# Two-way gated scan inside an encoder layer: inputs asked one place sooner, keys scaled in place, small copies on GpSimd, outputs scaled a place later

## The chip, the cores and the metric

The kernel runs on one core of one Trainium2 chip. The metric is device time in microseconds: the median of three runs, taken without the profiler. One further execution was profiled; all rows of the trace come from it.

The engines are TensorE (PE, with PEld for its weight loads), VectorE (DVE), ScalarE (ACT), GpSimd (POOL) and SyncE (SP). Each works through its own queue in order. SP issues most of the DMA transfers, ACT and GpSimd issue some.

## The reference

One layer of an encoder over 1024 positions of width 1024, all in float32. Cut to what matters:

```python
h = _rmsnorm(x, attn_norm_w)
glu_in, q, v, z_f, z_b, og, g_a, g_b = split(einsum("bsd,de->bse", h, w_in))
a = silu(layernorm(dwconv31(glu(glu_in)))) @ conv_pw_w
o = _bi_hgrn2(q, v, z_f, z_b, lb_fwd, lb_bwd)      # 8 heads of 128
b = (rms_per_head(o) * norm_w * silu(og)) @ hgrn_o_w
x = x + (sigmoid(g_a) * a + sigmoid(g_b) * b) @ w_out
x = x + conv_glu_ffn(rmsnorm(x)) ; out = rmsnorm(x)
```

The scan, in each direction and for each head, with `f = lb + (1 - lb) * sigmoid(z)` clamped to [1e-6, 1] and the key `k = (1 - lb) * sigmoid(-z)`:

```python
S_t = diag(f_t) S_{t-1} + k_t v_t^T
o_t = S_t^T (silu(q_t) * 128**-0.5)
```

The outputs of the forward and the backward scan are added.

## The kernel before

Every large product is done as three passes of float32r matmuls (`mm3`, lines 148 to 150: high by high, high by low, low by high), 128x128 weights against 128x512 activations, contracted over 128 at a time. TensorE's order is the order of the program text. The other engines' queues, SP's and GpSimd's transfers among them, are ordered before the launch by a scheduler that works with estimated costs and with the waits on tiles and pages (a page is one buffer of a tile's ring); instructions that are pinned keep their program order.

The stage around the change is the scan, which runs while the last columns of the input projection and the convolution's output product go on as a stream of dense pieces (`dense`). Work is cut into 16 half-heads: item i is head i // 2, half i % 2, with 512 positions on the free axis, 128 channels on the partitions. For each item:

- `scan_inputs(i)` (lines 1150 to 1166) loads q and two gate inputs z, makes from each z on ACT the key `kG = sigmoid(-z)` (L1162), `sigmoid(z)` (L1163) and `f` (L1164), and clamps f on DVE (L1165). Rings: q 2 pages, f 2, kG 3, z 3. The scale of the keys, `(1 - lb) * 128**-0.5`, comes back as `kscale`, not yet applied.
- `scan_base` is a generator of five steps. The first (lines 1221 to 1246) applies the key scale: `k_d`, the sum of the two scaled keys, by L1223 and L1224, and four half-width products of q, scale and f by L1229, into Q1 and qF. ACT copies kG in woven order (L1175) for the first level; then the keys and queries are doubled: at block size h each is multiplied by the product of the gates of the neighbouring block (`tt`, all recorded at L1143). Later steps do sizes 2, 4, 8 and 16 and issue the first levels of the score matrix on PE (L1194, bank sc).
- `scan_levels` yields three times: levels 8 and 16 (L1194, bank ob) and block 32 (L1284); then nothing; then block 64, after which ACT copies the scores into S (L1312), and four transfers of 16 KB, issued by ACT, put the diagonal 32x32 blocks D into S (L1314).
- `scan_states` yields twice: PE transposes kG (L1324), ACT copies them into kT (L1326), PE makes the states (L1333), and DVE chains the forward ones (L1339, L1341).
- The outputs of a head are a stream called `pending`, which runs during the next head: backward states (L1426); output products of half 0 (L1374), their copy on ACT and the sums of squares (L1379); the same of half 1, then on GpSimd the mean and the power to -0.5 (L591, L592, tile ors); an empty step; scaling on ACT of half 0, then half 1 (L1393, eight instructions of a quarter half); transposes and gating of half 0, then half 1 (L1400, L1402), stored to DRAM, or, for the last head, split into two parts for the output product.

The order is written out in the loop of lines 1449 to 1490. After each of an item's five yields `between(n)`, n = 0 to 4, runs: these are the five places. A place advances the dense stream by 1.77 pieces on average (a piece is six matmuls), `pending` by one step and the base of the next item (n below 4) or the one after it (n = 4) by one step. The inputs of item i + 2 are asked at the start of item i, that is, behind place 4 of item i - 1. Before the loop items 0 and 1 are asked, seven dense pieces follow, and then the steps of item 0's base with dense pieces between them.

Behind the loop `TAIL` gives the last head's outputs six steps with dense pieces between them; then come the loads of the other heads' outputs for half 0, one more step, the rest of the dense stream, the loads for half 1 and the last step. The output product `o_jobs` follows, head by head, so that the last head's first half is its eighth operand.

Of the kernel before, what the change touches and what calls it, by code (L numbers as in the profile page):

```python
# [18 lines left out]
P = 128  # L19
# [12 lines left out]
H = 512  # L32
# [5 lines left out]
def view(t, off, dims):  # L38

    return bass.AP(  # L40
        tensor=t.tensor,
        offset=t.offset + off,
        ap=[list(t.ap[0])] + [list(d) for d in dims],
    )
# [3 lines left out]
def tile_hybrid_encoder(  # L48
# [45 lines left out]
    def nm(s):  # L94
        uid[0] += 1
        return f"{s}_{uid[0]}"
# [6 lines left out]
    def page(pool, tag, bufs, dt=F32):  # L103
        return pool.tile([P, H], dt, tag=tag, name=nm(tag), bufs=bufs)
# [1046 lines left out]
    def scan_inputs(i):  # L1151


        h, half = divmod(i, 2)
        q = page(hp, "q", 2)
        f = hp.tile([P, 2, H], F32, tag="f", name=nm("f"), bufs=2)
        kG = hp.tile([P, 2, H], F32, tag="kG", name=nm("kG"), bufs=3)
        nc.sync.dma_start(q, d_q[h][half])
        for d in range(2):
            z = page(hp, "zi", 3)  # L1160
            nc.sync.dma_start(z, d_z[d][h][half])
            A.activation(kG[:, d, :], z, AF.Sigmoid, scale=-1.0)  # L1162
            A.activation(z, z, AF.Sigmoid)  # L1163
            A.activation(f[:, d, :], z, AF.Identity, scale=oml_of(d, h), bias=lb_of(d, h))  # L1164
        V.tensor_scalar(f, f, MIN_FORGET, 1.0, op0=ALU.max, op1=ALU.min)  # L1165
        return q, f, kG, kscale[:, h : h + NH + 1 : NH]
# [49 lines left out]
    def scan_base(ins):  # L1216


        q, f, kG, ks = ins
        qF = hp.tile([P, 2, H], F32, tag="qF", name=nm("qF"), bufs=4)  # L1220
        D_t = hp.tile([P, 4, 32], F32, tag="D", name=nm("D"), bufs=3)
        k_d, Q1 = page(hp, "A", 8), page(hp, "A", 8)
        V.tensor_scalar(k_d, kG[:, 1, :], ks[:, 1:2], None, op0=ALU.mult)  # L1223
        V.scalar_tensor_tensor(k_d, kG[:, 0, :], ks[:, 0:1], k_d, op0=ALU.mult, op1=ALU.add)  # L1224
        A1 = woven(kG, 1)
        odd = H // 2

        def gated(to, at, t, d):
            V.scalar_tensor_tensor(  # L1229
                view(to, at, [[2, odd]]),  # L1230
                view(q, t, [[2, odd]]),
                ks[:, d : d + 1],
                view(f, d * H + t, [[2, odd]]),
                op0=ALU.mult,
                op1=ALU.mult,
            )

        for t in range(2):
            gated(Q1, t, t, 1 - t)
        for t in (1, 0):  # L1240
            gated(qF, (1 - t) * H + t, t, t)
        double_keys(kG, f, 1)
        double_queries(qF, pairs(Q1, 1, 0), f, 1)
        tb = totals(f, 1)
        yield
        A2, Q2 = woven(kG, 2), woven(qF, 2)
        double_keys(kG, tb, 2)
        double_queries(qF, pairs(qF, 2), tb, 2)
        tb = totals(tb, 2)
        A4, Q4 = woven(kG, 4), woven(qF, 4)  # L1250
        yield
        b = bank("sc")
        for n, (k_t, q_t) in enumerate(((k_d, q), (A1, Q1), (A2, Q2), (A4, Q4))):
            level(slot(b, n), k_t, row(q_t))
        double_keys(kG, tb, 4)
        double_queries(qF, pairs(qF, 4), tb, 4)
        tb = totals(tb, 4)
        A8, Q8 = woven(kG, 8), woven(qF, 8)
        yield
        A.copy(D_t, near(slot(b, 3)))  # L1260
        for n, m in enumerate((m_d, m_1, m_2)):
            V.copy_predicated(D_t, over(m), near(slot(b, n)))
        double_keys(kG, tb, 8)
        double_queries(qF, pairs(qF, 8), tb, 8)
        tb = totals(tb, 8)
        A16, Q16 = woven(kG, 16), woven(qF, 16)
        yield
        double_keys(kG, tb, 16)
        double_queries(qF, pairs(qF, 16), tb, 16)
        tb = totals(tb, 16)  # L1270
        yield qF, kG, tb, D_t, A8, Q8, A16, Q16

    def scan_levels(base, S_t, Tt):


        qF, kG, tb, D_t, A8, Q8, A16, Q16 = base

        def blocks(b, h):

            for c in range(0, H, P):  # L1280
                for s0 in range(0, P, h):
                    t0 = s0 ^ h
                    d = s0 // h % 2
                    T.matmul(  # L1284
                        b[s0 : s0 + h, c + t0 : c + t0 + h],
                        kG[:, d, c + s0 : c + s0 + h],
                        qF[:, 1 - d, c + t0 : c + t0 + h],
                        start=True,
                        stop=True,
                    )  # L1290

        def double(tb, h, to=None):
            double_keys(kG, tb, h)
            double_queries(qF, pairs(qF, h), tb, h)
            return totals(tb, h, to)

        b = bank("ob")
        level(slot(b, 0), A8, row(Q8))
        level(slot(b, 1), A16, row(Q16))
        S_b = bank("sc")  # L1300
        for at, g, _ in each():
            T.matmul(S_b[g, at : at + 32], none, none, start=True, stop=True)
        blocks(S_b, 32)
        for n, m in enumerate((m_8, m_16)):
            V.copy_predicated(D_t, over(m), near(slot(b, n)))
        tb = double(tb, 32)
        yield
        yield
        b = S_b
        blocks(b, 64)  # L1310
        double(tb, 64, view(Tt, 0, [[4, 2], [1, 4]]))
        A.copy(S_t, c4(b))  # L1312
        for g in range(0, P, 32):
            nc.scalar.dma_start(S_t[g : g + 32, :, g : g + 32], D_t[g : g + 32])  # L1314
        yield

    def scan_states(i, kG, v, Tt, Sf, Sb):
# [38 lines left out]
    def scan_outputs(h, kept, Sf, Sb):  # L1356


        ons, gates = [], []
        ss = cp.tile([P, 2, 4], F32, name=nm("oss"), tag="oss", bufs=2)  # L1360
        rs = cp.tile([P, 2, 4], F32, name=nm("ors"), tag="ors", bufs=2)
        for half in range(2):
            S_t, v, qF = kept[half]
            o = bank("ob")
            for c in range(4):
                sl = slice(c * P, (c + 1) * P)
                g = half * 4 + c
                terms = [(S_t[:, c, :], v[:, c, :])]
                if g > 0:
                    terms.append((qF[:, 1, sl], Sf[half][:, c, :]))  # L1370
                if g < 7:
                    terms.append((qF[:, 0, sl], Sb[half][:, c, :]))
                for n, (l, r) in enumerate(terms):
                    T.matmul(o[:, sl], l, r, start=(n == 0), stop=(n == len(terms) - 1))  # L1374
            on = tmp()
            A.copy(on, o)
            for c in range(4):
                junk = hp.tile([P, DK], F32, tag="jk", name=nm("jk"), bufs=1)
                A.activation(  # L1379
                    junk, on[:, c * P : (c + 1) * P], AF.Square, accum_out=ss[:, half, c : c + 1]  # L1380
                )
            ons.append(on)
            gates.append(page(hp, "og", 2))
            nc.sync.dma_start(gates[half], d_og[h][half])
            if half == 0:
                yield
        rstd_small(rs, ss, DK)
        yield
        yield
        for half in range(2):  # L1390
            for c in range(4):
                sl = slice(c * P, (c + 1) * P)
                A.activation(  # L1393
                    ons[half][:, sl], ons[half][:, sl], AF.Copy, scale=rs[:, half, c : c + 1]
                )
            yield
        for half in range(2):
            b = bank("tr")
            for c in range(4):
                T.transpose(b[:, c * P : (c + 1) * P], ons[half][:, c * P : (c + 1) * P], ident)  # L1400
            bt = ev()
            V.scalar_tensor_tensor(bt, b, vec("hn", h), gates[half], op0=ALU.mult, op1=ALU.mult)  # L1402
            if h == NH - 1:
                bm[h][half] = split(hx(), hx(), bt, V)
            else:
                nc.sync.dma_start(d_bm[h][half], bt)
            yield
# [35 lines left out]
    NI = 2 * NH  # L1443
    cur = Base(scan_inputs(0))
    ahead = Base(scan_inputs(1))
    dense.fill(7)
    for pieces in (3, 4, 4, 3, 0):
        cur.step(1)
# [3 lines left out]
    for h in range(NH):  # L1452
# [4 lines left out]
        for half in range(2):  # L1457
            i = 2 * h + half
            base = cur.result()
            following = Base(scan_inputs(i + 2)) if i + 2 < NI else None  # L1460

            def between(n):
                dense.fill(FILL)
                pending.fill(1)
                step_of = ahead if n < 4 else following
                if step_of is not None:
                    step_of.step(1)
# [577 lines left out]
```

## Time and profile before

| | us |
|---|---|
| runs, without the profiler | 1736.55, 1735.89, 1734.44 (median 1735.89) |
| the profiled execution | 1732.47 |
| its span, first to last instruction | 1730.7 |
| TensorE busy | 1702.4 |
| VectorE busy | 1257.2 |
| ScalarE busy | 824.4 |
| GpSimd busy | 170.6 |

A row of the timeline gives the start in us, the length, engine, line, operation, tiles written and read, shape and count; in square brackets the idle time of the engine just before it, and what ended that. A row of a group of instructions gives the busy time and the mean of one in ns, then the idle time before them. A row of one line's instructions gives the shortest, the median and the longest in ns, and the first and the last start. Matmuls overlap, so the length of one is longer than its step from the last. A 128x512 matmul has a length of 390 ns in the trace.

### The profile page before, as it was taken

Reading aid. Unit: us, or ns where it says so; the run is one execution under the profiler, and the core shown is the slowest. Engines: PE = TensorE matmul, PEld = TensorE weight load, DVE = VectorE, ACT = ScalarE, POOL = GpSimd, SP = SyncE. Lnnn points to the kernel's source line nnn. Section 1 sums busy time; section 2 is a strip of 40 time slices with the busy share of each in tenths; the row PEclk is TensorE's granted clock in tenths of the full one; section 3 lists DMA queues with packets and bytes.
Section 4 is the critical chain, followed back from the end, with each engine's and each line's share of the span. In section 5 each row is a group of like instructions: output and inputs, shape, how many; then the busy total and the mean of one; then the engine's idle time right before and its main releaser. Section 6 shows DMA issues by size and latency. Waiting matters only on the chain. (4 is left out here: it accounts for less than half of the span.)

```text
span 1730.7 us, 30713 instructions
## 1 busy us (share of the span) xinstructions
PE 1702.4 (98%) x11902; PEld 1415.8 (82%) x11902; DVE 1257.2 (73%) x1953; ACT 824.4 (48%) x1544; POOL 170.6 (10%) x185
## 2 busy tenths in 40 slices
PE   8999999999999999999999999999999999999997
PEld 6878887888788888888888888888888888888787
DVE  4599999746778888878657466767776877657864
ACT  7444433334566777776442245444434443542334
POOL 2211111100000000000000002011111111000110
PEclk9999999999999999999999999999999999999999
DMA  8768887855673434435579466577777877783842
GB/s 285 241 170 187 197 193 187 210 160 156 207 226 102 133 127 133 127 115 186 176 249 331 153 205 206 145 155 149 174 172 156 183 170 162 231 263 102 213 93 98
DMA packets 343752, 308.28 MB, mean 178 GB/s; under 512 B 25262, under 2 KB 255798, under 8 KB 343606
## 3 DMA queue, kind: packets, MB, share of 16 engines
q1 hardware_dynamic: 289590, 267.51, 48.7%
q0 software_dynamic: 44800, 37.76, 15.2%
q10 hardware_dynamic: 9216, 1.05, 0.4%
q8 instruction: 93, 1.52, 0.3%
q14 instruction: 53, 0.43, 0.1%
HBM read 201.40 MB, written 87.03 MB: 167 GB/s over the span
## 5 line engine op out<-in xcount | busy, mean ns | idle before, releaser
L148 PE MATMUL mm<-hx,wp 128*128 128x512 f32 x1068 | 427.3, 400 | 2.7 <-ACT tm L850 1.5
L150 PE MATMUL mm<-hx,wp 128*128 128x512 f32 x1068 | 417.5, 391 | 1.2 <-DVE wp L124 1.2
L149 PE MATMUL mm<-hx,wp 128*128 128x512 f32 x1068 | 416.6, 390 | 0.0
L124 ACT CAST wp<-wr 128x1024 fp32r<-128x1024 f32 (+2 forms) x147 | 147.3, 1002 | 254.3 <-PE mm L149 111.0
L150 PEld LDWEIGHTS mm<-hx,wp 128*128 128x128 f32 x1068 | 200.6, 188 | 46.2 <-DVE wp L124 3.4
L148 PEld LDWEIGHTS mm<-hx,wp 128*128 128x128 f32 x1068 | 200.9, 188 | 45.4 <-DVE ev L799 2.2
L149 PEld LDWEIGHTS mm<-hx,wp 128*128 128x128 f32 x1068 | 201.0, 188 | 39.8 <-issue 1.0
L124 DVE TENSOR_TENSOR wp<-wr,wp 128x1024 fp32r<-128x1024 f32 (+2 forms) x145 | 169.5, 1170 | 71.2 <-ACT wp L124 64.8
L1038 DVE SCALAR_TENSOR_TENSOR acc<-gl,v_b,acc 128x1024 f32<-128x1024 f32 x120 | 149.1, 1279 | 0.4
L439 ACT COPY su<-mm 128x512 f32<-128x512 f32 x82 | 47.7, 581 | 56.9 <-PE mm L150 56.3
L1143 DVE TENSOR_TENSOR qF<-qF,tb 128x512 f32<-128x512 f32 x96 | 65.7, 686 | 6.9 <-ACT A L1175 6.7
L148 PE MATMUL tr<-hx,wp 128*128 128x512 f32 x180 | 70.5, 392 | 0.0
L124 ACT CAST wq<-sw 128x1024 fp32r<-128x1024 f32 x41 | 43.2, 1054 | 56.8 <-PE mm L149 46.2
L150 PE MATMUL tr<-hx,wp 128*128 128x512 f32 x180 | 70.1, 389 | 0.0
L149 PE MATMUL tr<-hx,wp 128*128 128x512 f32 x180 | 70.0, 389 | 0.0
L1641 DVE SCALAR_TENSOR_TENSOR tm<-gp,v_a,tm 128x512 f32<-128x512 f32 x88 | 66.0, 750 | 3.9 <-ACT tm L1639 2.0
L1143 DVE TENSOR_TENSOR kG<-kG,tb 128x512 f32<-128x512 f32 x96 | 65.1, 685 | 0.5 <-ACT A L1175 0.4
L148 PE MATMUL mm<-hy,wp 128*128 128x512 f32 x164 | 64.2, 391 | 0.0
L148 PE MATMUL sc<-hy,wq 128*128 128x512 f32 x164 | 64.2, 391 | 0.0
L150 PE MATMUL sc<-hy,wq 128*128 128x512 f32 x164 | 63.8, 389 | 0.0
L149 PE MATMUL mm<-hy,wp 128*128 128x512 f32 x164 | 63.8, 389 | 0.0
L149 PE MATMUL sc<-hy,wq 128*128 128x512 f32 x164 | 63.8, 389 | 0.0
(372 smaller groups left out, 3616.5 us busy)
## 6 DMA issues: line engine op xcount, KB each, us to landing
wr<-in_w_in_dram SPq DMA_DIRECT2D x48, 512.0 KB, 4.8
wr<-in_ffn_w_up_dram SPq DMA_DIRECT2D x22, 512.0 KB, 4.0
sw<-in_w_in_dram SPq DMA_DIRECT2D x38, 256.0 KB
d_g<-ft SPq DMA_DIRECT2D x38, 256.0 KB, 2.8
sw<-in_ffn_w_up_dram SPq DMA_DIRECT2D x38, 256.0 KB, 4.5
sw<-in_ffn_w_up_dram POOLq DMA_DIRECT2D x19, 512.0 KB, 8.1
wr<-sw POOLq DMA_DIRECT2D x32, 256.0 KB, 3.4
wr<-wr POOLq DMA_DIRECT2D x32, 256.0 KB, 4.0
```

Source lines behind the costliest of these rows:

```text
L124: parts = A.copy(hi, src), eng.tensor_tensor(lo, src, hi.bitcast(F32), op=ALU.subtract)
L148: T.matmul(acc, whi[:, k, :], ahi, start=first, stop=False, skip_group_check=again)
L149: T.matmul(acc, whi[:, k, :], alo, start=False, stop=False, skip_group_check=again)
L150: T.matmul(acc, wlo[:, k, :], ahi, start=False, stop=last, skip_group_check=again)
L439: A.copy(t, acc)
L1038: V.scalar_tensor_tensor(acc, g[:, k : k + S], tap(k), acc, op0=ALU.mult, op1=ALU.add)
L1143: V.tensor_tensor(o, a, b, op=op)
L1641: V.scalar_tensor_tensor(c, g[:, o + k : o + k + H], vec("fdw", k * NF + j), c, op0=ALU.mult, op1=ALU.add,)
```

## The change

- Before the loop, the inputs of item 2 are asked too, ahead of the seven dense pieces. In the loop, the inputs of item i + 3 are asked at place 4 of item i, ahead of what that place runs. The ring of kG has four pages instead of three, that of q three instead of two.
- The key scale is applied to kG itself, in place, by two VectorE instructions, ahead of the woven copy; `k_d` is then a plain sum, and the first queries are two full-width products of q and f without the scale. The scaled keys go on into the levels and the states; the queries are no longer scaled.
- The four small transfers from D to S are issued by GpSimd instead of ACT.
- The outputs have a second empty step ahead of their scaling, so scaling, transposes and gating come one place later; behind the loop both halves' transposes of the last head come behind the rest of the dense stream.

```diff
-        q = page(hp, "q", 2)
+        q = page(hp, "q", 3)
-        kG = hp.tile([P, 2, H], F32, tag="kG", name=nm("kG"), bufs=3)
+        kG = hp.tile([P, 2, H], F32, tag="kG", name=nm("kG"), bufs=4)
...
+        for d in range(2):
+            V.tensor_scalar(kG[:, d, :], kG[:, d, :], ks[:, d : d + 1], None, op0=ALU.mult)
         k_d, Q1 = page(hp, "A", 8), page(hp, "A", 8)
-        V.tensor_scalar(k_d, kG[:, 1, :], ks[:, 1:2], None, op0=ALU.mult)
-        V.scalar_tensor_tensor(k_d, kG[:, 0, :], ks[:, 0:1], k_d, op0=ALU.mult, op1=ALU.add)
+        tt(k_d, kG[:, 0, :], kG[:, 1, :], ALU.add)
         A1 = woven(kG, 1)
         odd = H // 2
-        def gated(to, at, t, d):
-            V.scalar_tensor_tensor(
-                view(to, at, [[2, odd]]),
-                view(q, t, [[2, odd]]),
-                ks[:, d : d + 1],
-                view(f, d * H + t, [[2, odd]]),
-                op0=ALU.mult,
-                op1=ALU.mult,
-            )
-        for t in range(2):
-            gated(Q1, t, t, 1 - t)
-        for t in (1, 0):
-            gated(qF, (1 - t) * H + t, t, t)
+        tt(
+            pairs(Q1, 1, 0),
+            view(q, 0, [[1, 2], [2, odd], [1, 1]]),
+            view(f, H, [[1 - H, 2], [2, odd], [1, 1]]),
+        )
+        tt(
+            view(qF, 1, [[H - 1, 2], [2, odd]]),
+            view(q, 1, [[-1, 2], [2, odd]]),
+            view(f, H + 1, [[-(H + 1), 2], [2, odd]]),
+        )
...
         for g in range(0, P, 32):
-            nc.scalar.dma_start(S_t[g : g + 32, :, g : g + 32], D_t[g : g + 32])
+            G.dma_start(S_t[g : g + 32, :, g : g + 32], D_t[g : g + 32])
...
         rstd_small(rs, ss, DK)
         yield
         yield
+        yield
         for half in range(2):
...
     ahead = Base(scan_inputs(1))
+    coming = scan_inputs(2)
     dense.fill(7)
...
-            following = Base(scan_inputs(i + 2)) if i + 2 < NI else None
+            following = Base(coming) if i + 2 < NI else None
+            coming = None
             def between(n):
+                nonlocal coming
+                if n == 4 and i + 3 < NI:
+                    coming = scan_inputs(i + 3)
                 dense.fill(FILL)
                 pending.fill(1)
```

## The prediction

> **What bounds it now.** I read the page's engine lines first, then the timeline of TensorE (PE) through the scan stage for every row that shows idle time before it, then the same moments on VectorE (DVE) and ScalarE (ACT).
>
> ```profile
> span 1730.7 us, 30713 instructions
> PE 1702.4 (98%) x11902; PEld 1415.8 (82%) x11902; DVE 1257.2 (73%) x1953; ACT 824.4 (48%) x1544; POOL 170.6 (10%) x185
> 480.00:905.00 425.00, 417.05 (x6100) 354.48 (x6099) 329.05 (x712) 282.93 (x636) 14.69 (x16) 1.00 0.48 154
> ```
>
> TensorE is the bound, and no matmul is added or removed. What the edit can win is TensorE's idle time in the stage that it touches: 425.00 - 417.05 = 7.95 us (third row: window, its length, busy time of PE, PEld, DVE, ACT, POOL, then granted clock, DMA share, GB/s). In the scan itself that is seven gaps:
>
> ```profile
> 588.00 0.66 PE L1324 MATMUL tr<-ident,kG 128*128 128x128 f32 x4 [1.72 <-DVE kG L1143]
> 627.97 0.46 PE L1194 MATMUL sc<-A,A 128*32 128x32 f32 x32 [0.26 <-ACT A L1175]
> 680.76 1.16 PE L1333 MATMUL sc<-v,kT 128*128 128x128 f32 x8 [0.63 <-ACT kT L1326]
> 722.14 1.11 PE L1324 MATMUL tr<-ident,kG 128*128 128x128 f32 x4 [2.24 <-DVE kG L1143]
> 764.17 0.46 PE L1194 MATMUL sc<-A,A 128*32 128x32 f32 x32 [1.01 <-ACT A L1175]
> 813.65 0.66 PE L1324 MATMUL tr<-ident,kG 128*128 128x128 f32 x4 [0.72 <-DVE kG L1143]
> 818.23 1.16 PE L1333 MATMUL sc<-v,kT 128*128 128x128 f32 x8 [0.73 <-ACT kT L1326]
> 722.00:724.00 2.00, 1.86 (x9) 1.87 (x10) 2.00 (x5) 0.13 (x1) 0.00 (x0) 0.50 0.96 270
> 724.00:726.00 2.00, 2.00 (x8) 1.58 (x8) 2.00 (x7) 1.83 (x4) 0.00 (x0) 0.66 1.05 309
> ```
>
> They sum to 7.31 us. Behind the longest the granted clock falls to 0.50 and 0.66, which costs 1.86 x 0.50 + 2.00 x 0.34 = 1.6 us more. So about 8.9 us are there to be had. From 588.00 to 813.65 there are ten half-heads: 22.6 us each, or 4.5 us for each of the five places of a half-head.
>
> Who is late before each gap? Four of the gaps follow a stretch in which DVE stood at the clamp of the gates:
>
> ```profile
> DVE f L1165 <- ACT f L1164: 17.9, 8, 5.5
> 578.04 0.70 DVE L1165 TENSOR_SCALAR f<-f 128x1024 f32<-128x1024 f32 x1 [2.00 <-ACT f L1164]
> 712.32 0.70 DVE L1165 TENSOR_SCALAR f<-f 128x1024 f32<-128x1024 f32 x1 [2.67 <-ACT f L1164]
> 759.17 0.69 DVE L1165 TENSOR_SCALAR f<-f 128x1024 f32<-128x1024 f32 x1 [5.51 <-ACT f L1164]
> 803.18 0.69 DVE L1165 TENSOR_SCALAR f<-f 128x1024 f32<-128x1024 f32 x1 [4.35 <-ACT f L1164]
> 703.56 0.59 ACT L1326 COPY kT<-mm 128x512 f32<-128x512 f32 x1
> 708.11 0.70 ACT L1393 ACTIVATE tm<-tm,ors 128x128 f32<-128x128 f32 x2 [1.33 <-POOL ors L592]
> 709.67 0.62 ACT L1162 ACTIVATE kG<-zi 128x512 f32<-128x512 f32 x1
> 711.48 0.80 ACT L1164 ACTIVATE f<-zi,lbw 128x512 f32<-128x512 f32 x1
> ```
>
> The first row (waiting line, releaser, total, times, longest) says 17.9 us in eight waits. The pairs are 578.04 and the gap at 588.00, 712.32 and 722.14, 759.17 and 764.17, 803.18 and 813.65: DVE runs its queue in order, stands idle for the gates, then works without a break and still reaches the doubling of kG late. On ACT the second gate's chain (709.67 to 711.48) sits behind L1393, the scaling of outputs, which itself stood 1.33 us for GpSimd's power; and the gates only start around kT (703.56), the copy of the transposes that free a page of kG. The two L1333 gaps have another cause:
>
> ```profile
> 676.53 2.55 ACTq L1314 DMA_DIRECT2D S<-D  x4
> 679.18 1.05 ACT L124 CAST wp<-wr 128x1024 fp32r<-128x1024 f32 x1 [2.68 <-DMA S<-D]
> 680.13 0.58 ACT L1326 COPY kT<-tr 128x512 f32<-128x512 f32 x1
> ```
>
> ACT spends 2.55 us issuing four small transfers, a cast is behind them, and kT behind that.
>
> **The change part by part.** DVE, ACT and the DMA queues run in an order fixed before the launch, and the trace of before cannot show the new one; so each part gets the two ends of its price.
>
> *Gates sooner, fourth kG page, third q page.* Gates of item i+3 are asked ahead of the last place of item i, one place (4.5 us) before the old spot, and the fourth page takes away the wait on the transposes. The waits of 2.00, 2.67 and 4.35 us fit into one place; 5.51 does not, by 1.0. Ends: nothing, or the four gaps and the clock, 1.72 + 2.24 + 1.01 + 0.72 + 1.6 = 7.3 us. I take 6.8, leaving half of the gap at 764. The moved step issues, for each half-head, one q load, two z loads, six activations and one clamp; the loads pass others on SP's queue, where the third q page removes a wait rather than adding one. f keeps two pages, but the page that item i+3 takes was last read one half-head earlier.
>
> *At the start* the same step for item 2 now stands ahead of the first dense pieces:
>
> ```profile
> 502.97 0.46 PE L1194 MATMUL sc<-q,A 128*32 128x32 f32 x32
> 502.01 0.63 ACT L1175 COPY A<-qF 128x512 f32<-128x512 f32 x1
> ```
>
> The first level on PE (502.97) comes 0.33 us after its last operand (502.64). Six activations, by 709.67 and 711.48 above, are at most 2 x (0.62 + 0.62 + 0.80) = 4.1 us, so the ends are 0 and 3.8 us of idle PE. I take 0.3, near the good end: item 2's z pages (a ring of three) come free only as items 0 and 1 finish their gates, so its activations can hardly overtake the first chain.
>
> *Transfers to GpSimd.* 64 issues of 2.55 / 4 = 0.64 us leave ACT. The trace shows no 16 KB transfer on GpSimd; the nearest rows are its accumulating ones:
>
> ```profile
> L301 POOL DMA_DIRECT2D wr<-sw x32: 856/892/911, 125.0 to 1460.5; - x32
> L592 POOL TENSOR_TENSOR ors<-ors,mhalf x8: 1635/1635/1642, 572.3 to 875.8; 128x8 f32<-128x8 f32 x8
> 854.53 2.56 ACTq L1314 DMA_DIRECT2D S<-D  x4
> 870.46 0.39 PE L1374 MATMUL ob<-v,S 128*128 128x128 f32 x2
> ```
>
> Four at 0.89 are 3.6 us per half-head on an engine that is busy 14.69 of 425 us. The tightest use of S is the last: 870.46 - 854.53 = 15.9 us after the issue, so landing hides unless the four take over four times as long. Queued behind them is the power pair of the outputs (1.64 us and a short scale), for which ACT waits at L1393. Worth: between 0 and the L1333 gaps, 0.63 + 0.73 = 1.36. I take 1.36, because nothing else of length stands ahead of kT there.
>
> *Outputs scaled a place later* gives that power 4.5 us against its 3.6 us of new neighbours; I cost it at nothing in the loop. At the tail it moves both output transposes behind the last dense piece:
>
> ```profile
> 882.74 0.60 PE L1400 MATMUL tr<-ident,tm 128*128 128x128 f32 x4
> 888.67 0.60 PE L1400 MATMUL tr<-ident,tm 128*128 128x128 f32 x4
> 893.78 0.69 DVE L124 TENSOR_TENSOR hx<-ev,hx 128x512 fp32r<-128x512 f32 x1
> 894.82 0.39 PE L148 MATMUL mm<-hx,wp 128*128 128x512 f32 x1
> 896.14 0.75 DVE L1402 SCALAR_TENSOR_TENSOR ev<-tr,v_a,og 128x512 f32<-128x512 f32 x1 [1.67 <-DMA d_a<-ev]
> ```
>
> The split of the last head's first half ends at 894.47 for a matmul at 894.82: 0.35 us of room. Its transposes go from 882.74 to about 888.7, so its L1402 falls into a full stretch of DVE. Best end 0; worst, it is as late as the second half is now (896.14 + 0.75, then a cast and a subtraction of 0.69 each: 898.3), a gap of 3.5 us. I take 1.0, nearer the good end, since it no longer holds a page that a later piece waits for.
>
> *Arithmetic of the first step.*
>
> ```profile
> L1223 DVE TENSOR_SCALAR A<-kG,kscale 128x512 f32<-128x512 f32 x16 | 7.7, 480 | 4.9 <-ACT kG L1162 4.9
> L1224 DVE SCALAR_TENSOR_TENSOR A<-kG,kscale,A 128x512 f32<-128x512 f32 x16 | 12.0, 747 | 0.2
> L1229 DVE SCALAR_TENSOR_TENSOR A<-q,kscale,f 128x256 f32<-128x256 f32 x32 | 14.4, 481 | 0.0
> L1143 DVE TENSOR_TENSOR qF<-A,f 128x512 f32<-128x512 f32 x16 | 11.0, 688 | 0.0
> ```
>
> Out: 480 + 747 + 4 x 481 = 3151 ns. In: 2 x 480 + 3 x 688 = 3024 ns. DVE gains 0.13 us per half-head, 2 us in all, off the path: nothing. But the first copy on ACT now waits for the two scalings, 0.96 us that were not ahead of it. With the gates a place early that hides; without, it is 0.96 on an item that is already late.
>
> *The new order's own misses.* The old order has seven gaps in sixteen half-heads with a median of 0.73 us; I charge one of that size.
>
> Sum: 6.8 + 1.36 - 0.3 - 1.0 - 0.73 = 6.1 us. The profiled execution took 1732.47 (1.77 around its span), so 1726.4 by that count; the median shown is 3.42 above it, which gives **1729.8**.
>
> Two pages speak to this. The Trainium skill (TensorE: Matmul & The Clock Gate, What's actually happening) puts the half clock after an idle window of about 3.4 us; here a gap of 2.24 us shows it, so the row decides. By the page the 1.6 us would not be there, and the sum would be 4.5. The other page stands with its rival.
>
> **Rivals.**
> (a) *Everything goes*: no gap, no dip, nothing new, 8.9 us: 1727.0. For it: every gap has its cause among the moved parts, but for the cast behind 627.97. Against: the tail's 0.35 us.
> (b) *The gates are still late.* ACT gets room but keeps them behind other work: only L1333's gaps and part of the others go, about 3 us, 1732.9. This is also the case in which the change does not do what it says: the loop asks one place sooner, not three. For it: 5.51 us exceeds a place.
> (c) *Slower: the early step displaces the current item.* Its DVE work (clamp 0.69 and 3.0 us) lands ahead of the 64-doubling, and the transposes wait in every second half-head as at 588.00: 8 x 1.72 = 13.8, with a dip behind two, 3.2. Against 8.9 that is +8: 1744. It decides from 5.2 such gaps on (8.9 / 1.72). Against: DVE is busy 329.05 of 425 us.
> (d) *Slower: GpSimd holds the outputs up.* If each small transfer takes 1.8 us, twice the row, four and the power (8.8 us) overrun the place by 4.3; ACT stands that long in eight heads, against 1.5 now (12.1 us in eight waits):
>
> ```profile
> ACT tm L1393 <- POOL ors L592: 12.1, 8, 2.0
> ```
>
> If half of the 2.8 us more reaches PE, that is 8 x 1.4 = 11.2 us; the gates behind L1393 stay late, so of the gains only 1.36 is left: 1746. The row of 856 to 911 ns, taken beside a DVE busy most of that stage, is against it. The Trainium skill (SBUF — State Buffer, SBUF: two separate sides) gives a reason for it: GpSimd cannot write descriptors while DVE runs certain fast operations. The narrow spread of that row shows no such blocking.
>
> **How the numbers follow.** Forecast 0.48, (a) 0.17, (b) 0.20, (c) 0.11, (d) 0.04. About 0.2%, 3.5 us, is what a measurement of this kernel can tell from no change: the limits are 1732.4 and 1739.4. Forecast (1727.5 to 1732.3), (a), and a tenth of (b) are faster: 0.67. The rest of (b), 0.18, is same; (c) and (d) are slower, 0.15. The range leaves out the two slow cases and the edge of (a): 1726 to 1738.
>
> **What would show it.** Right: DVE's wait for ACT f falls from 17.9 to under 5 us; the L1324 gaps and the clock dip go; no kT behind transfers; L1393 no longer waits for ors; PE busy within 3 us of the 425. Wrong: a PE gap before 503, one behind the tail's transposes for hx, L1324 gaps in more than five half-heads, or GpSimd's small transfers well over 0.9 us.

## The result and the profile after

| | median us | lowest to highest | runs |
|---|---|---|---|
| before | 1734.67 | 1732.92 to 1736.55 | 7 |
| after | 1740.72 | 1739.04 to 1744.06 | 7 |

The ratio is 1.0033 [1.0022, 1.0044]: slower by 6.05 us, where 6.1 us faster was forecast, and outside the range. The profiled execution of after is the 1744.06, the highest of its seven; that of before, 1732.47, lies below all seven of before.

From the page of after: the span, the engines, and the group of GpSimd's small transfers (count, total us, mean ns).

```profile
span 1742.3 us, 30769 instructions
PE 1706.2 (98%) x11902; PEld 1417.6 (81%) x11902; DVE 1254.8 (72%) x1937; ACT 826.5 (47%) x1544; POOL 206.2 (12%) x249
L1310 POOL DMA_DIRECT2D S<-D x64 | 35.4, 559 | 289.7 <-ACT S L1308 157.1
```

Idle TensorE is 1742.3 - 1706.2 = 36.1 us against 1730.7 - 1702.4 = 28.3 before. Its busy time has grown by 3.8 us with the same 11902 matmuls, so the clock was lower somewhere. The windows of after say where (length, busy PE, PEld, DVE, ACT, POOL, granted clock, DMA share, GB/s):

```profile
480.00:905.00 425.00, 410.70 (x6068) 348.61 (x6067) 329.06 (x700) 285.43 (x637) 50.22 (x80) 0.99 0.49 157
500.00:510.00 10.00, 7.58 (x151) 5.99 (x151) 8.12 (x17) 10.00 (x19) 0.00 (x0) 0.90 0.67 204
510.00:520.00 10.00, 10.00 (x94) 8.02 (x95) 8.51 (x20) 6.41 (x11) 0.00 (x0) 0.93 0.33 91
530.00:880.00 350.00, 347.88 (x5445) 298.77 (x5444) 274.27 (x601) 237.22 (x558) 49.09 (x79) 1.00 0.44 141
890.00:900.00 10.00, 2.34 (x8) 1.05 (x7) 6.07 (x9) 4.02 (x7) 0.00 (x0) 0.85 0.89 305
900.00:910.00 10.00, 8.45 (x24) 6.39 (x25) 6.94 (x11) 2.59 (x5) 0.00 (x0) 0.63 1.03 341
```

And TensorE's timeline, every row of the stage with over 0.3 us of idle before it:

```profile
505.82 0.46 PE L1194 MATMUL sc<-A,A 128*32 128x32 f32 x32 [0.84 <-ACT A L1175]
507.86 0.62 PE L1194 MATMUL sc<-A,A 128*32 128x32 f32 x32 [1.58 <-ACT A L1175]
592.67 0.63 PE L1320 MATMUL tr<-ident,kG 128*128 128x128 f32 x4 [1.45 <-ACT S L1308]
636.86 0.63 PE L1320 MATMUL tr<-ident,kG 128*128 128x128 f32 x4 [0.33 <-ACT S L1308]
723.31 0.63 PE L1320 MATMUL tr<-ident,kG 128*128 128x128 f32 x4 [0.32 <-DVE kG L1143]
887.18 0.50 PE L150 MATMUL mm<-hx,wp 128*128 128x512 f32 x1 [0.55 <-DVE wp L124]
891.84 0.50 PE L148 MATMUL mm<-hx,wp 128*128 128x512 f32 x1 [0.73 <-ACT hx L124]
892.82 0.50 PE L149 MATMUL mm<-hx,wp 128*128 128x512 f32 x1 [0.48 <-DVE hx L124]
901.54 0.80 PE L148 MATMUL mm<-hx,wp 128*128 128x512 f32 x1 [7.99 <-ACT hx L124]
```

(L1320 is the L1324 of before, L1390 the L1393, L1308 the L1312, L1399 the L1402.) What the reader is to see is a stage that won in its middle and lost at both ends:

| place | before, us lost | after, us lost |
|---|---|---|
| gaps in the scan's middle | 7.31 | 1.45 + 0.33 + 0.32 = 2.10 |
| lowered clock at 722 to 726 | 1.6 | 0 |
| start: gaps, and clock 7.58 x 0.10 + 10.00 x 0.07 | 0 | 2.42 + 1.46 |
| tail: gaps, and clock 2.34 x 0.15 + 8.45 x 0.37 | 0.34 | 9.75 + 3.48 |
| sum | 9.25 | 19.21 |

The clock's share is an estimate, busy time times what the clock lacks: a window's mean clock counts idle time too, and in windows of 2 us the start's comes to 1.7 us and the tail's to 2.9. The difference, 10.0 us, is most of the 11.6 us between the two spans. That the medians lie only 6.05 apart while the profiled executions lie 11.6 apart is the spread of single executions (one the lowest of its kernel, one the highest); the experiments below therefore go by ratios, each with the kernel before run on the same chip.

At the tail, the timelines of after on VectorE and ScalarE:

```profile
889.03 1.41 DVE L1399 SCALAR_TENSOR_TENSOR ev<-tr,v_a,og 128x512 f32<-128x512 f32 x2
891.16 1.29 ACT L124 CAST hx<-tm 128x512 fp32r<-128x512 f32 x2 [1.83 <-DMA tm<-d_bm]
893.58 1.25 ACT L124 CAST hx<-tm 128x512 fp32r<-128x512 f32 x2 [1.12 <-DMA tm<-d_bm]
897.67 1.32 ACT L124 CAST hx<-tm 128x512 fp32r<-128x512 f32 x2 [2.84 <-DMA tm<-d_bm]
899.69 1.27 ACT L124 CAST hx<-tm 128x512 fp32r<-128x512 f32 x2 [0.71 <-DMA tm<-d_bm]
900.87 1.13 ACT L124 CAST hx<-ev 128x512 fp32r<-128x512 f32 x2
```

The last head's gated outputs are finished at 890.44 (889.03 + 1.41). Their split, the `hx<-ev` row, starts at 900.87. ACT had nothing else to do for most of that time: it stood in its queue for loads of the other heads. Of the eight casts shown as `hx<-tm`, the first is the last of half 0; the other seven are half 1, and they come first in that queue. TensorE's matmul at 901.54 waits for the first of the two casts.

At the start, ScalarE's timeline of after:

```profile
497.75 1.26 ACT L1162 ACTIVATE kG<-zi 128x512 f32<-128x512 f32 x2 [1.15 <-DMA zi<-d_z]
505.11 0.66 ACT L1175 COPY A<-qF 128x512 f32<-128x512 f32 x1
507.18 0.62 ACT L1175 COPY A<-qF 128x512 f32<-128x512 f32 x1
```

And the counterpart of the first copy before (that of the second is the row at 502.01 in the prediction):

```profile
499.87 0.68 ACT L1175 COPY A<-qF 128x512 f32<-128x512 f32 x1
```

The two woven copies of qF, for which the first levels on TensorE wait, start at 505.11 and 507.18; before, they started at 499.87 and 502.01. That is 5.2 us later, while TensorE itself reached the first level only 1.25 us later (504.22 beside 502.97). Gates stand ahead of them on ACT, from 497.75 to 504.64.

### The profile page after: what moved, and what is told of

It reads as the page before. It is cut to its first block, busy times and chain, and to the rows that moved or that the text cites. A ratio compares the mean times of both kernels' runs of the same rounds, so it can differ in the third digit from the quotient of the medians.

```text
span 1742.3 us, 30769 instructions
## 1 busy us (share of the span) xinstructions
PE 1706.2 (98%) x11902; PEld 1417.6 (81%) x11902; DVE 1254.8 (72%) x1937; ACT 826.5 (47%) x1544; POOL 206.2 (12%) x249
## 5 line engine op out<-in xcount | busy, mean ns | idle before, releaser
L1310 POOL DMA_DIRECT2D S<-D x64 | 35.4, 559 | 289.7 <-ACT S L1308 157.1
L148 PE MATMUL sc<-hy,wq 128*128 128x512 f32 x164 | 64.2, 391 | 0.0
L150 PE MATMUL sc<-hy,wq 128*128 128x512 f32 x164 | 63.8, 389 | 0.0
```

The lines of the kernel that those rows point to most:

```text
L148: T.matmul(acc, whi[:, k, :], ahi, start=first, stop=False, skip_group_check=again)
L150: T.matmul(acc, wlo[:, k, :], ahi, start=False, stop=last, skip_group_check=again)
L1310: G.dma_start(S_t[g : g + 32, :, g : g + 32], D_t[g : g + 32])
```

## The experiments

Runs made together share a chip and its runs of before. All ratios are to before, as is the 1.0033 of after. Most kernels ran eight to ten times; the two best, one line of the change and that line with GpSimd's transfers, ran four times each.

### The tail

**After with a short tail.**

```diff
-        yield            # the third, after
+        if h < NH - 1:
+            yield
```

> The changed kernel, but the second empty step ahead of the scaling is left out for the last head alone, so the last head's transposes stand where they stood before the change. Theory (the loss sits behind the loop: the split of the last head's first half is queued behind the seven loads of half 1 on ScalarE and VectorE; 7.99 + 0.73 + 0.48 us of TensorE idle and about 3 us at a lowered clock): 12 us less than the changed kernel's 1740.7, so 1728 to 1730, and no TensorE gap over 1 us between 880 and 910 us. Rival (the loss is in the scan itself, from GpSimd's transfers or the new order): within 3 us of 1740.7.

Measured: 1731.14 us (1727.63 to 1741.2), ratio 0.9967 [0.9951, 0.9984]. Giving the last head its old places takes 0.66% off after, 11.5 us, and turns the change into a gain. The longest gap left from 880 to 910 is 1.14 us.

**After with the loads asked last.** Nothing but the place of one statement behind the loop changes:

```diff
     dense.drain()
-    bm_loads(1)
     pending.drain()
+    bm_loads(1)
```

> The changed kernel with one pair of statements swapped behind the loop: the last head's transposes and split come ahead of the seven loads of half 1, not behind them; the transposes stay behind the last dense piece. Theory (queue behind the loads): the gap of 7.99 us and its lowered clock go, 1728 to 1732, though the loads of half 1 now come later and may cost up to 3 us in the second half of the first output product. Rival (the transposes themselves are too late, or the pages they hold slow the loads of half 0): the gap stays above 4 us, 1736 or more.

Measured: 1734.06 us, ratio 0.9973 [0.9961, 0.9985]. Its timelines on TensorE and ScalarE:

```profile
889.32 0.80 PE L148 MATMUL mm<-hx,wp 128*128 128x512 f32 x1 [1.99 <-ACT hx L124]
888.65 0.62 ACT L124 CAST hx<-tm 128x512 fp32r<-128x512 f32 x1 [1.95 <-DMA tm<-d_bm]
889.17 1.14 ACT L124 CAST hx<-ev 128x512 fp32r<-128x512 f32 x2
```

The transposes are as late in the text as in after, yet the 7.99 us gap is 1.99: the split now stands right behind the last cast of half 0 (888.65), no longer behind the seven of half 1 as well. So most of the gap came from the place in the queue, not from the transposes being late. By the ratios the swap takes 0.60% off after, 10.4 us; the time still lies 2 us above the 1728 to 1732 that I had expected.

**Before with late outputs.** The third `yield` alone, last head included, in the kernel before.

```diff
         rstd_small(rs, ss, DK)
         yield
         yield
+        yield
```

> The kernel of before with the second empty step ahead of the scaling as its only edit. Theory: it loses the tail's price, 9 to 13 us: 1744 to 1748, with a TensorE gap of several us for the last head's split behind the loop; the gaps inside the scan stay near 7 us in sum. Rival (the extra place costs nothing by itself and the loss needs the other parts): 1733 to 1736.

Measured: 1739.72 us, ratio 1.0013 [1.0002, 1.0024]. One line of the change makes the same hole, 7.35 us of idle TensorE up to the matmul at 897.64. But the expectation failed otherwise: the time is 4 us below its 1744, and the scan's gaps did not stay near 7 us; idle TensorE from 530 to 880 is 350 - 347.61 = 2.39 us. The same line that makes the hole behind the loop mends the loop.

### The start

**After with item 2 asked in the loop.**

```diff
-    coming = scan_inputs(2)      # ahead of the loop
+    coming = None
...
+            if i == 0:
+                coming = scan_inputs(2)
             following = Base(coming) if i + 2 < NI else None
```

> The changed kernel with item 2's gates asked inside item 0 and nothing else undone, so the late tail stays. If start and tail add up: the start's 2.4 us of idle and some 1.6 us of clock go, 4 us of about 1737.7, from 1.0033 to about 1.001, with the tail's gap of 8 us still there. If the items behind come late instead (the asking is moved, and its loads with it): 1.002 or more, and new gaps in items 2 to 4.

Measured: 1738.44 us, ratio 1.0009 [0.9996, 1.0023]; no gap near 505, and the tail's gap still there, 7.15 us up to 896.66. From 1.0033 that is 0.24%, 4.2 us, beside 3.9 us in the table above.

**Both undone** (this edit and the short tail).

> The changed kernel without the second empty step for the last head, and with the inputs of item 2 asked where they were asked before, at the start of item 0. Theory (two losses, behind the loop 12 us and at the start 2.42 us of idle with some 1.6 us of lowered clock): 1723 to 1727, with no TensorE gap at the first levels near 503 us. Rival (the start's gap comes from elsewhere, such as the scaling ahead of the woven copy): no better than the kernel with the tail alone undone.

Measured: 1728.83 us, ratio 0.9957 [0.9942, 0.9972]. What is left of the change gains 0.43%, 7.5 us. Beside the run with item 2 alone undone, the tail is worth 0.52%, 9.0 us. Beside the run with the short tail alone (0.9967), the start is worth only 0.10%, 1.7 us, and the two intervals overlap: by time alone the rival is not excluded. The trace does that, TensorE being busy for all of 500 to 510.

### What makes the gain in the middle

**Only GpSimd's transfers**, in the kernel before.

```diff
-            nc.scalar.dma_start(S_t[g : g + 32, :, g : g + 32], D_t[g : g + 32])
+            G.dma_start(S_t[g : g + 32, :, g : g + 32], D_t[g : g + 32])
```

> The kernel of before with the four small transfers issued by GpSimd as its only edit. Theory (ScalarE's issue time stands ahead of kT): the two gaps at L1333, 1.36 us, go and the others stay, so 1 to 2 us faster than before. Rival (GpSimd's queue holds the outputs up): slower by several us, with ScalarE's wait for ors well over 12 us.

Measured: 1735.47 us, ratio 0.9988 [0.9979, 0.9997]: 2.1 us. By the interval that is 0.5 to 3.6 us. Both gaps at L1333 are gone.

**Only the gates**: asked early with item 2 ahead of the loop, fourth key page, third query page.

```diff
+                if n == 4 and i + 3 < NI:
+                    coming = scan_inputs(i + 3)
...
+    coming = scan_inputs(2)
```

> The kernel of before with the early inputs and the third q and fourth kG page as its only edits. Theory of the prediction (the gates sit late because they are asked late): VectorE's wait for f falls under 6 us, the four gaps of 5.7 us and the lowered clock go, and the start costs 2 to 4 us as in the changed kernel: 3 to 6 us faster than before. Rival (the place of the scaling of outputs on ScalarE alone set the gates back, since the later outputs alone had cut the scan's gaps to 2.4 us): the gaps stay near 7 us, and the start's loss makes it 2 to 4 us slower.

Measured: 1736.08 us, ratio 0.9997 [0.9982, 1.0012], neither the gain of the theory nor the loss of the rival. Two waits of this run from 505 to 870, a row of its TensorE, and its window at the start:

```profile
DVE f L1165 <- ACT f L1164: 1.9, 3, 1.0
DVE qF L1143 <- ACT A L1175: 17.6, 17, 3.6
769.93 0.66 PE L1324 MATMUL tr<-ident,kG 128*128 128x128 f32 x4 [1.52 <-DVE kG L1143]
500.00:510.00 10.00, 7.75 (x156) 6.17 (x155) 8.02 (x15) 10.00 (x19) 0.00 (x0) 1.00 0.66 207
```

The second of these waits before, over the same stretch:

```profile
DVE qF L1143 <- ACT A L1175: 6.7, 11, 2.3
```

VectorE's wait at the clamp, the prediction's culprit, has all but vanished (16.8 us before), and gaps at the transposes of kG remain. The wait has moved: VectorE now stands for the woven copies, 17.6 us where it was 6.7. The start has nearly the gaps of after (0.67 + 1.58 = 2.25 us, up to 507.55), but in this execution the clock stayed at 1.00 behind them.

**The same gates, item 2 inside the loop.**

```diff
-    coming = scan_inputs(2)
+    coming = None
...
+            if i == 0:
+                coming = scan_inputs(2)
```

> The kernel before with the gates asked early inside the loop only (item 2's inside item 0), with the fourth key page and the third query page. If early gates bring the gain by themselves and item 2's start hid it: no gap near 505, scan gaps under 3 us, ratio 0.995 to 0.997. If not: gaps of 4 to 6 us as with item 2's start, ratio 0.998 to 1.000.

Measured: 1733.07 us, ratio 0.9974 [0.9965, 0.9983]. So early gates do gain, 4.5 us, and item 2's start had hidden it. But the gaps are smaller, not gone: idle TensorE from 530 to 880 is 350 - 345.28 = 4.72 us, 7.55 before. Whether the earlier asking or the extra pages bring the gain was not tried apart. In this run's timelines on ScalarE and VectorE:

```profile
708.85 2.16 ACT L1393 ACTIVATE tm<-tm,ors 128x128 f32<-128x128 f32 x7 [1.63 <-POOL ors L592]
712.06 0.64 ACT L1175 COPY A<-qF 128x512 f32<-128x512 f32 x1
712.73 0.69 DVE L1143 TENSOR_TENSOR qF<-qF,tb 128x512 f32<-128x512 f32 x1 [2.82 <-ACT A L1175]
```

The gates that VectorE needs next are no longer behind the scalings L1393, but a woven copy is, and VectorE stands 2.82 us for that copy instead; the transposes at 721.41 still wait 0.92 us. What is behind L1393 in ACT's queue is held, in this trace as in that of before.

**Only the arithmetic of the first step** (the diff's hunk at L1223 alone).

```diff
+        for d in range(2):
+            V.tensor_scalar(kG[:, d, :], kG[:, d, :], ks[:, d : d + 1], None, op0=ALU.mult)
...
-        for t in range(2):
-            gated(Q1, t, t, 1 - t)
+        tt(pairs(Q1, 1, 0), ...)
```

> The kernel of before with the new first step alone (keys scaled in place, plain products). Theory: nothing by itself, within 2 us of before. Rival (the woven copy that now waits for the scaling lengthens the chain): 3 us slower or more, with TensorE gaps at L1194.

Measured: 1737.91 us, ratio 1.0006 [0.9995, 1.0017]: nothing that can be told.

**Gates in the loop, and the arithmetic**: the two edits above together.

> The run of the gates in the loop, and the first step's arithmetic with it. It differs from the run without the later outputs by the transfers alone (on ScalarE here). If gates and arithmetic together carry that run's 0.9964: 0.996 to 0.998, with gaps at the matmuls that follow kT (0.2 to 1 us each) as the transfers' share. If the transfers are what makes it: 0.999 to 1.001, gaps over 5 us.

Measured: 1732.35 us, ratio 0.9978 [0.9966, 0.999]; beside 0.9974 the arithmetic adds nothing.

**Everything but the later outputs** (no third `yield`, item 2 in the loop): the last run plus the transfers, in the terms of after:

```diff
         yield
         yield
-        yield
...
-    coming = scan_inputs(2)
+    coming = None
...
+            if i == 0:
+                coming = scan_inputs(2)
```

> The changed kernel without its later outputs, and with item 2's gates asked inside item 0: what is left is the gates asked early, the fourth key page and third query page, the arithmetic and GpSimd's transfers. Theory that the later outputs alone carry the gain: ratio 0.998 to 1.001, scan gaps of 4 us or more though VectorE's wait at the gates' clamp is gone. The prediction's theory (gates late cause the gaps): ratio 0.995 to 0.997, scan gaps under 2.5 us and no dip of the clock.

Measured: 1731.96 us, ratio 0.9964 [0.995, 0.9977]; the transfers add 0.14%, beside 0.12% alone, though the intervals of this run and the last overlap. My theory that the later outputs alone carry the gain falls with this run: gates and transfers gain without them.

### Outputs a place later

**Before with late outputs and the short tail.** One line of the change, for all heads but the last.

```diff
         yield
         yield
+        if h < NH - 1:
+            yield
         for half in range(2):
```

> The kernel of before with the second empty step ahead of the scaling, but not for the last head. Theory (the later outputs free the gates on ScalarE inside the scan, and cost only behind the loop): the scan's gaps near 2.4 us as with the step in every head, no gap of several us behind the loop: 5 to 7 us faster than before. Rival (the scan's gain belonged to another order that the missing last step undoes): within 2 us of before.

Measured: 1727.01 us (1725.62 to 1728.22), ratio 0.994 [0.9924, 0.9957]: 10.4 us faster than before (7.5 to 13.2 by the interval, which holds the 8.9 us that the middle had to give). The two traces show 7.5 us of that in the middle, 7.55 - 1.66 of gaps and the 1.6 of lowered clock, while their spans lie only 4.5 us apart (1730.7 and 1726.2), the trace of before being faster than any of its runs; where the rest comes from is open. Its window of the scan's middle, its waits from 505 to 870, and its timelines on ScalarE, VectorE and TensorE around the place of the old 2.24 us gap (L1395 is the L1393 of before, L1404 the L1402):

```profile
530.00:880.00 350.00, 348.34 (x5439) 298.34 (x5438) 276.17 (x612) 237.23 (x560) 14.67 (x16) 1.00 0.47 146
DVE f L1165 <- ACT f L1164: 17.8, 10, 3.5
707.04 0.80 ACT L1164 ACTIVATE f<-zi,lbw 128x512 f32<-128x512 f32 x1
708.22 0.69 ACT L1395 ACTIVATE tm<-tm,ors 128x128 f32<-128x128 f32 x2
709.92 1.28 ACT L1395 ACTIVATE tm<-tm,ors 128x128 f32<-128x128 f32 x4
707.88 0.69 DVE L1165 TENSOR_SCALAR f<-f 128x1024 f32<-128x1024 f32 x1 [3.25 <-ACT f L1164]
716.77 0.68 DVE L1143 TENSOR_TENSOR kG<-kG,tb 128x512 f32<-128x512 f32 x1
698.55 0.60 PE L1324 MATMUL tr<-ident,kG 128*128 128x128 f32 x4
718.78 0.74 DVE L1404 SCALAR_TENSOR_TENSOR ev<-tr,v_a,og 128x512 f32<-128x512 f32 x1
```

And before, the same waits and the same stretch on ScalarE, VectorE and TensorE:

```profile
DVE f L1165 <- ACT f L1164: 16.8, 7, 5.5
709.07 0.69 ACT L1393 ACTIVATE tm<-tm,ors 128x128 f32<-128x128 f32 x2
710.19 0.39 ACT L1393 ACTIVATE tm<-tm,ors 128x128 f32<-128x128 f32 x1
719.00 0.75 DVE L1402 SCALAR_TENSOR_TENSOR ev<-tr,v_a,og 128x512 f32<-128x512 f32 x1
721.39 0.69 DVE L1143 TENSOR_TENSOR kG<-kG,tb 128x512 f32<-128x512 f32 x1
701.10 0.60 PE L1324 MATMUL tr<-ident,kG 128*128 128x128 f32 x4
```

VectorE waits as long at the clamp as ever (17.8 us beside 16.8), and idle TensorE is 350 - 348.34 = 1.66 us. The new trace is already 2.55 us ahead here (the transposes of the half-head before start at 698.55 and 701.10), so times are counted from those transposes. The wait at the clamp is harmless because it now ends 9.33 us behind them (707.88), where it ended at 11.22 (712.32): six of the eight scalings run behind the second f (708.22, 709.92), where before five ran ahead of it (708.11 to 710.19, f at 711.48). The doubling of kG that the next transposes need comes at 18.22 instead of 20.29, and the product of the outputs, at 17.90 before, has moved behind it, to 20.23. From the clamp to that doubling VectorE takes 8.89 us instead of 9.07, so nearly all of the 2.07 us won lies ahead of the clamp, on ScalarE.

Which of the two moves counts was tried one at a time. **Late transposes, scaling at the old place:**

```diff
                 A.activation(... scale=rs[:, half, c : c + 1])
             yield
+        if h < NH - 1:
+            yield
```

> The kernel before with one yield more between the scaling of the outputs and their transposes (all heads but the last): ScalarE scales at the old place, so the gates stay behind it; only the transposes and VectorE's product with the gate of the outputs come one place later. Theory V (what counts is that this product no longer runs on VectorE ahead of the 64-doubling of kG): the scan's gaps, 7.3 us from 530 to 880, fall to under 3 us, VectorE's wait at the gates' clamp stays near 17 us, ratio 0.994 to 0.997. Theory S (what counts is that ScalarE's scalings no longer stand between the two gate chains): the gaps stay over 5 us, ratio 0.998 to 1.002.

Measured: 1737.62 us, ratio 0.9992 [0.9981, 1.0004]. TensorE's timeline keeps the old gap of 2.24 us at 2.30 (and the one of 1.72); behind it, in this execution, the clock did not fall:

```profile
722.99 0.63 PE L1324 MATMUL tr<-ident,kG 128*128 128x128 f32 x4 [2.30 <-DVE kG L1143]
724.00:726.00 2.00, 2.00 (x11) 1.63 (x10) 2.00 (x5) 1.27 (x3) 0.00 (x0) 1.00 0.77 208
```

**Late scaling of the first half, transposes at the old place:**

```diff
+        if h < NH - 1:
+            yield
         for half in range(2):
...
-            yield
+            if half == 1 or h == NH - 1:
+                yield
```

> The kernel before with only ScalarE's scalings later: the first half's one place later, so that both halves are scaled in the same place, and the transposes and the product on VectorE stay where they were (all heads but the last). Theory V: the gaps of the scan stay over 5 us, ratio 0.998 to 1.002. Theory S: they fall under 3 us, ratio 0.994 to 0.997. If each does a part, both this run and the one of the late transposes lie near 0.997.

Measured: 1731.87 us, ratio 0.996 [0.9949, 0.9971], with its window of the middle:

```profile
530.00:880.00 350.00, 345.32 (x5424) 295.79 (x5423) 276.09 (x611) 236.74 (x559) 14.66 (x16) 1.00 0.45 142
```

The first half's scaling, moved alone, is worth 0.40%, the product alone nothing that can be told; both halves' scaling and the product together 0.60%. The time speaks for theory S; idle TensorE here is 4.68 us, which neither theory had, between the 7.55 of before (from the same window) and the 1.66. Before's row:

```profile
530.00:880.00 350.00, 342.45 (x5398) 293.59 (x5396) 271.70 (x603) 234.61 (x554) 14.69 (x16) 1.00 0.44 141
```

**Late outputs, short tail, GpSimd's transfers.** Two parts of the change, without the early gates and the arithmetic: the edits of the two runs that tried them alone.

> The kernel before with two parts of the change: the outputs one place later in all heads but the last, and GpSimd's small transfers. If the parts add up, 0.994 less 0.001, that is 0.993 (1725.5 beside a before of 1737.5), with no gap behind a cast that waits for transfers. If GpSimd's transfers only move the order about, 0.993 to 0.997 and new gaps of other lines.

Measured: 1727.11 us (1725.02 to 1728.78), ratio 0.9929 [0.9905, 0.9952]. It is faster than before and after, and cannot be told from the one-line version.

| kernel | ratio to before |
|---|---|
| after | 1.0033 |
| after, start undone | 1.0009 |
| after, tail undone | 0.9967 |
| after, both undone | 0.9957 |
| gates in the loop alone | 0.9974 |
| later outputs alone, short tail | 0.994 |
| later outputs, short tail, transfers | 0.9929 |

The gains don't add: gates (0.26%) and later outputs (0.60%) remove the same gaps, and with both and the transfers it is 0.43%. That 0.9957 and 0.994 differ is not shown, since their intervals overlap. Why both together come out no better than the later outputs alone wasn't tried beyond this; what after keeps in the middle is mostly its gap of 1.45 us behind the scores' copy on ScalarE, which the later outputs alone don't show.

## Why the prediction was wrong

**What failed** is the costing of the two ends of the stage. With the start at the 3.9 us of the trace for 0.3 and the tail at 9.0 to 12.7 for 1.0, the prediction's own sum of +6.1 becomes -5.5 to -9.2; measured is -6.05. The range for the tail is that of three pairs of runs which differ in the last head's extra place alone: 0.52% and 0.66% above, and 0.73% between the two kernels of before with late outputs (1.0013 and 0.994).

- **Tail: 1.0 us taken, 3.5 called the worst; 9.0 to 12.7.** The step that failed is "worst, it is as late as the second half is now". It counted how late the transposes and VectorE's product become, and took the split to follow at once. It did not ask what stands ahead of that split on ScalarE. The extra place moves it behind the loads for half 1, and each of their splits waits for a transfer. The swap of two statements showed this. The lowered clock behind the hole (0.85, 0.63) had no term either.
- **Start: 0.3 taken, 3.8 the bad end; 2.42 of gaps and 1.46 of clock in the trace, 1.7 to 4.2 by three pairs of runs** (0.10% and 0.24% above, 0.23% between the two runs of the gates). The step that failed is that item 2's activations "can hardly overtake the first chain", because their pages come free late. A wait for `zi` was there (1.15 us), but the activations stood ahead of the copies all the same, and in an in-order queue that wait held the copies too. The clock's part is not a fixed price: the run of the gates alone had nearly these gaps and no lowered clock.
- **Gates sooner: 6.8 taken; 4.5 us alone in the loop** [3.0 to 6.1 by the interval]. The direction was right, the cause half right. VectorE's wait at the clamp was read as the cause of four gaps. Two runs separate them: early gates took that wait from 16.8 to 1.9 and left gaps; later outputs left it at 17.8 and took the gaps. The obstacle was the block of scalings that waits for GpSimd's power, which the prediction had quoted (1.33 us at 708.11) but put second: moving half of that block was worth 0.40%. Whether its wait or its own time counts was not tried.
- **Outputs a place later: nothing in the loop taken.** Alone it removes almost all the gaps, 0.60%. The prediction asked only whether GpSimd would be in time, not what ScalarE's eight scalings had stood in front of.
- **GpSimd's transfers: 1.36 us taken; 2.1** alone (0.5 to 3.6) and 0.14% on top of the others. The cause was right, both L1333 gaps went. One takes 559 ns (634 at most) where 856 to 911 was taken, so rival (d) has nothing to rest on.
- **Arithmetic: nothing**, and nothing that can be told (0.9 us faster to 3.0 slower by the interval). VectorE's idle time did move to its first instruction, as the waits of after from 480 to 915 show:

```profile
DVE kG L1223 <- ACT kG L1162: 15.3, 7, 4.7
DVE f L1165 <- ACT f L1164: 2.7, 3, 1.2
```

The promised sign, f's wait under 5 us, came true on a line that now only follows another wait. The other one, that L1390 would no longer wait for ors, is false: it waits 12.6 us, against 12.1 before, in a middle whose gaps are down to 2.10. Two signs of being wrong came: idle TensorE at the first levels, and the gap for hx behind the tail's transposes; TensorE's busy time is 14.3 us short of the 425, not 3.

- **The new order's own misses: 0.73 taken; 2.10** (1.45 + 0.33 + 0.32).

The middle as a whole was forecast at 6.8 + 1.36 - 0.73 = 7.4 us, and after with both ends undone gains 7.5. That the sizes agree is partly luck: the gates were taken too high, and the later outputs, which alone remove almost all the gaps, at nothing. Of the rivals, (c) had the sign, but its place was the loop, where one half-head has a gap of its size (1.45 us) and none of the others over 0.33; the displaced item was item 0. No rival held the tail.

## What to carry to other kernels

Before moving a step in an in-order queue, list what it will stand behind and what will stand behind it, at the first and the last turn of the loop above all: what is free in the middle of a stream can be the bound where the stream begins or ends. An engine's idle time ahead of a late operation is not yet the cause; take away the wait alone and see whether the gap goes. Undo the parts of a mixed change one at a time: here one line of it, with the last head left out, is worth more than the whole.

## What the runs showed of the hardware

How long a gap must be for the granted clock to fall is not fixed in these traces. In after, two gaps of 0.84 and 1.58 us with 0.46 us of matmuls between them gave 0.90 in their window of 10 us and 0.93 in the next; with the gates alone, gaps of 0.67 and 1.58 us left it at 1.00. The gap of 2.24 us in before halved it, one of 2.30 us with late transposes did not, and one of 1.45 us in after did not. A price put on the clock from one trace, like the 1.6 us of the prediction, holds for that execution.

A transfer of 16 KB that ScalarE issues in 0.64 us takes GpSimd 0.56, less than the 0.86 to 0.91 of its accumulating ones, beside a VectorE that is busy 329 of 425 us.

Single executions of one kernel lay up to 13.6 us apart (1727.63 to 1741.2, after with a short tail); the cause was not looked for.
